# A hybrid three-group encoder layer: the second group's V projection in 512-column matmuls over two token tiles by turns, later differential steps, and moved loads

## The chip, the core and the metric

The kernel runs on one core of one Trainium2 chip. The metric is the device time of one launch in microseconds (us); the median of the runs is quoted. The core has five engines that run their own instruction queues in order and meet at semaphores: TensorE (PE; its weight loads appear as PEld), VectorE (DVE), ScalarE (ACT), GpSimd (POOL) and SyncE (SP), which here only issues DMAs. ScalarE's queue issues a few DMAs too (rows with ACTq).

## The reference

Two layers over x (512 tokens of width 1024, float32). In each layer the input is normalised and projected once; the columns of that projection belong to three head groups: A (differential attention, with rotary embedding on q and k), B (stick-breaking attention), C (forgetting attention with a cumulative gate).

```python
h = rms_norm(x, g_pre)
p = h @ w_in
qa, ka, va, ga, qs, ks, vs, gs, qf, kf, vf, gf, ff = jnp.split(p, split_at, axis=-1)
qa = apply_partial_rope(qa...); ka = apply_partial_rope(ka...)
ya = merge(diff_attention(qa, ka, heads(va), lam, lambda_init, subln)) * jax.nn.silu(ga)
yb = merge(stick_breaking_attention(heads(qs), heads(ks), heads(vs))) * jax.nn.silu(gs)
yc = merge(forgetting_attention(heads(qf), heads(kf), heads(vf), cum_log_f)) * jax.nn.silu(gf)
y = jnp.concatenate([ya, yb, yc], axis=-1) @ w_out
return x + rms_norm(y, g_post)
```

## The kernel before

Every large product is made of three matmuls (`mm3`, L200 to L202): each operand is held as a rounded high part and a low remainder, and high by high, high by low and low by high are summed in PSUM. The transposed normalised input `hT` is cut once per layer. Each weight unit (512 KB, `raw`) is loaded by SP, ScalarE writes its high part (`hl`, L184), and GpSimd writes the low part (L190) in four pieces of 256 columns; `split_to` does this, unit by unit, and four `hl` buffers (`whl_p`) and three `raw` buffers go round. The matmul of L201 is the one that reads the low part of a V unit.

The order of all work is written out by a planner: `do(cost, fn)` puts a piece of TensorE's main stream at the planner's own clock `now`, `at(t, fn)` puts other work (evictions, attention steps, splits, loads) at a time of that clock, and in the end everything is sorted by that time and emitted, each engine taking its instructions in that order. The planner's times (in ns) are only a sort key. The weights of a unit are split at its time of use less its `lead`.

In each layer the groups come in the order a, c, b: V first, then q and k for four pairs. While TensorE projects one group, the attention steps of the group before it are threaded in (`steps`): during c's projection those of a (`step_a`, the differential steps), during b's those of c, and those of b run during the gate projections. A differential step writes two score tiles in PSUM (`s`, two buffers, L364), VectorE takes their minimum (`mn`, L389) and so frees them, ScalarE takes the exponential (L398).

For the third group (b), V is projected by `proj_V`: four weight units of 256 rows by 512 columns, 512-column matmuls, one token tile of 128 after the other. For a and c it is `proj_N`: two column halves of 256, each of two units. For group a's q and k, VectorE applies the rotary embedding first (L328 to L332), ScalarE then writes the high part of q or k (L344) and VectorE the low part (L349).

After the last projection the output projection runs in two column halves; its first half is kept in `acc` tiles in PSUM and multiplied by the post-norm weights `gain` (L791); the second half runs token tile by token tile, and the next layer's pre-norm (`pre_norm_stages`: squares, two scalings, two transposes `turn`) is threaded in at five offsets after each tile.

Of the kernel before, what the change touches and what calls it, by code (L numbers as in the profile page):

```python
# [10 lines left out]
F32 = mybir.dt.float32  # L11
# [49 lines left out]
def hybrid_kernel(ctx, tc, x, w_in, forget_bias, diff_lambda, diff_subln, w_out, pre_norm, post_norm, consts, out):  # L61
# [137 lines left out]
    def mm3(ps, lh, ll, rh, rl, first, last):  # L199
        nc.tensor.matmul(out=ps, lhsT=lh, rhs=rh, start=first, stop=False)  # L200
        nc.tensor.matmul(out=ps, lhsT=lh, rhs=rl, start=False, stop=False)  # L201
        nc.tensor.matmul(out=ps, lhsT=ll, rhs=rh, start=False, stop=last)  # L202
# [33 lines left out]
        for t, fn in done(st):  # L236
            at(now[0] + t, fn)

    def proj_V(k0, tt, hT, done):

        st = {}
        sl = slice(tt * 128, (tt + 1) * 128)

        def go(q):
            if q == 0:
                st["ps"] = pj_p.tile([128, S], F32, name="pj", tag="pj")
            h = hT()
            for kc in range(2 * q, 2 * q + 2):
                u = halves[k0 + q]["hl"][:, :, kc % 2]
                mm3(st["ps"], h[0][:, kc, sl], h[1][:, kc, sl], u[:, 0], u[:, 1], kc == 0, kc == KC - 1)  # L250

        for q in range(4):
            do(1296, lambda q=q: go(q))
        at(now[0], lambda: done(st["ps"]))


    def pre_norm_stages(st, tt, hT):
# [56 lines left out]
        t = qk_p.tile([128, 2, S], F32, name="gain", tag="kd")  # L314
        return [t[:, 0], t[:, 1]]

    def load_gain(g, src):
        for h, t in enumerate(g):
            nc.sync.dma_start(out=t, in_=src[h * S:(h + 1) * S].partition_broadcast(128))


    H = (slice(0, 64), slice(64, 128))
# [267 lines left out]
    def first_norm(L):  # L590
        def load(tt):
            st = L["st", tt]
            t = qk_p.tile([128, 2, S], F32, name="xl", tag="qd")
            nc.sync.dma_start(out=t.rearrange("p h c -> p (h c)"), in_=x[0, tt * 128:(tt + 1) * 128, :])
            st["x"] = [t[:, 0], t[:, 1]]
            st["g"] = L.get("g")

        def first_gain():

            row = pt1_p.tile([1, 2, S], F32, name="grow", tag="pT1")  # L600
            nc.scalar.dma_start(out=row.rearrange("p h c -> p (h c)"), in_=pre_norm[0:1])
            one = t1_p.tile([1, 128], F32, name="one", tag="on")
            nc.vector.memset(one, 1.0)
            L["g"] = []
            for h in range(2):
                ps = s_p.tile([128, S], F32, name="s", tag="s")
                nc.tensor.matmul(out=ps, lhsT=one, rhs=row[:, h], start=True, stop=True)
                L["g"].append(ps)

        for tt in range(NT):  # L610
            L["st", tt] = {}
        t = -40000
        at(t, lambda: nc.vector.memset(mhalf, -0.5))
        at(t, lambda: load(0))
        at(t, first_gain)
        at(t, lambda: load_to(1))
        at(t, load_ident)
        at(t, lambda: L["st", 0].update(g=L["g"]))
        at(t, lambda: load_to(2))
        at(t, lambda: load(1))  # L620
        at(t, lambda: load(2))
        at(t, lambda: load_to(3))
        at(-20000, lambda: load(3))
        at(-19000, load_consts)
        S_ = [pre_norm_stages(L["st", tt], tt, L["hT"]) for tt in range(NT)]
        for t, tt, j in ((-30000, 0, 0), (-29900, 0, 1), (-29800, 0, 2), (-28000, 0, 3), (-27900, 0, 4), (-27000, 1, 0),
# [3 lines left out]
            at(t, S_[tt][j])  # L630

    def plan_layer(l, L):
# [9 lines left out]
        for g in ("a", "c", "b"):  # L642
            base = G[g]
            c = dict(pairs=[{} for _ in range(4)], lc=lc)
            st = {}
            c["v"] = lambda st=st: st["v"]
            c["o"] = lambda st=st: st["o"]
            c["cs"] = cs[l]
            t0 = now[0]
            at(t0, lambda st=st: st.update(v=v_p.tile([128, NT, 512], F32, name="v", tag="v")))  # L650
            if prev is not None:
                pst, pc, pg = prev
                at(t0, lambda pst=pst: pst.update(o=o_p.tile([128, 4, S], F32, name="o" + pg, tag="o")))
                steps(step_a if pg == "a" else step_c, pc, t0 + (3518 if pg == "a" else 3191), 50075 if pg == "a" else 46774)
            order = [(u, tt) for u in range(2) for tt in range(NT)]
            if g == "a":
                order = [(0, 0), (0, 1), (0, 2), (1, 0), (1, 1), (1, 2), (0, 3), (1, 3)]
            ks = []
            if g == "b":
                order = []  # L660
                kv = add_v_unit(l, base + 1024)
                for h in range(4):
                    use(kv + h, now[0] + 1296 * h)
                for tt in range(NT):
                    proj_V(kv, tt, hT, lambda ps, st=st, tt=tt: nc.scalar.activation(out=st["v"][:, tt], in_=ps, func=AF.Copy))
            for u in range(2 if g != "b" else 0):
                ks.append(add_in_unit(l, base + 1024 + u * UW, 6144 if g == "a" and u == 0 else None))
            seen = set()
            for u, tt in order:
                ex = g == "a" and u == 0  # L670
                w = UW + (8 if ex else 0)
                if u not in seen:
                    seen.add(u)
                    use(ks[u], now[0])
                    use(ks[u] + 1, now[0] + 1300)
                    if g == "a" and u == 1:
                        halves[ks[u]]["lead"], halves[ks[u] + 1]["lead"] = 7500, 6500

                def done(pst, u=u, tt=tt, ex=ex, st=st, w=w):
                    def ev():  # L680
                        nc.scalar.activation(out=st["v"][:, tt, u * UW:(u + 1) * UW], in_=pst["ps"][:, 0:UW],
                                             func=AF.Copy)
                        if ex:
                            if "ff" not in ffd:
                                ffd["ff"] = lay.tile([128, 32], F32, name="ff", tag="ff")
                            nc.vector.tensor_copy(ffd["ff"][:, tt * 8:(tt + 1) * 8], pst["ps"][:, UW:w])
                    return [(0, ev)]
                proj_N(ks[u], w, tt, hT, done)
            if g == "a":
                at(now[0] + 2000, lambda: layer_consts(lcd, l))  # L690
                at(now[0] + 5000, lambda: ffd.update(lf=decay(ffd["ff"], lcd, l)))
                at(now[0] + 9000, lambda: decay_sum(ffd["lf"], l))
            sc = 0.125 if g == "b" else -0.125
            for u in range(2):
                for part in ("q", "k"):
                    k0 = add_in_unit(l, base + u * UW + (512 if part == "k" else 0))
                    use(k0, now[0])
                    use(k0 + 1, now[0] + 2600)
                    if g == "a" and u == 0 and part == "q":
                        for h in range(2):  # L700
                            halves[k0 + h].update(lead=2500, lo="both")
                    if g == "b" and u == 0 and part == "q":
                        for h in range(2):
                            halves[k0 + h]["lead"] = (3800, 5100)[h]
                    for cc in range(2):
                        keep = c["pairs"][2 * u + cc]
                        if part == "q":
                            proj_T(k0, cc, hT, lambda pst, keep=keep: qk_done(pst, g == "a", sc, keep, "q"))
                        else:
                            proj_T(k0, cc, hT, lambda pst, keep=keep: qk_done(pst, g == "a", 1.0, keep, "k"))  # L710
            prev = (st, c, g)
            ctxs[g] = (st, c)
# [83 lines left out]
        def new_post():  # L796
            t = qk_p.tile([128, 2, S], F32, name="gain", tag="qs")
            gains["post"] = [t[:, 0], t[:, 1]]
            load_gain(gains["post"], post_norm[l])
        at(now[0] - 9000, new_post)  # L800
        N = None
        if l + 1 < DEPTH:
            nx = {}
# [13 lines left out]
        for tt in range(NT):  # L817
# [41 lines left out]
            at(t, square)  # L859
            at(t + 1867, add)  # L860
            if N is not None:
                for d, fn in zip((2500, 4500, 4600, 7551, 8326), pre_norm_stages(st, tt, N["hT"])):
                    at(t + d, fn)
        return N

# [50 lines left out]
```

## Time and profile before

| what | value |
|---|---|
| median of 3 runs | 869.72 us (869.27 to 870.09) |
| profiled execution, device time | 870.16 us |
| its span, first to last instruction | 868.1 us |
| mean granted TensorE clock | 0.998 |
| TensorE busy | 852.5 us, 98% of the span, 4700 matmuls |
| VectorE, ScalarE, GpSimd busy | 57%, 55%, 52% |

The table says where to look: TensorE is busy for all but some 16 us of the span, so a change counts by what it does to TensorE's own instructions and to its few waits. A busy share of an engine beside it says little by itself.

### The profile page before, as it was taken

Reading aid. Unit: us, or ns where it says so; the run is one execution under the profiler, and the core shown is the slowest. Engines: PE = TensorE matmul, PEld = TensorE weight load, DVE = VectorE, ACT = ScalarE, POOL = GpSimd, SP = SyncE. Lnnn points to the kernel's source line nnn. Section 1 sums busy time; section 2 is a strip of 40 time slices with the busy share of each in tenths; the row PEclk is TensorE's granted clock in tenths of the full one; section 3 lists DMA queues with packets and bytes.
Section 4 is the critical chain, followed back from the end, with each engine's and each line's share of the span. In section 5 each row is a group of like instructions: output and inputs, shape, how many; then the busy total and the mean of one; then the engine's idle time right before and its main releaser. Section 6 shows DMA issues by size and latency. Waiting matters only on the chain.

```text
span 868.1 us, 13536 instructions
## 1 busy us (share of the span) xinstructions
PE 852.5 (98%) x4700; PEld 711.0 (82%) x4700; DVE 496.4 (57%) x1143; ACT 475.9 (55%) x1056; POOL 447.7 (52%) x678
## 2 busy tenths in 40 slices
PE   7999999999999999999999999999999999999997
PEld 5988998888878787788898889888888787877885
DVE  5378656544555777623653875664445477774322
ACT  4344667757775556633334356675677756664310
POOL 3366554645544548770364664556274544678301
PEclk9999999999999999999999999999999999999999
DMA  7354323432523321237253452325244422122522
GB/s 236 96 163 134 94 81 91 118 101 80 154 76 105 85 61 53 71 117 247 96 177 98 122 146 74 98 73 162 59 131 113 120 54 71 49 81 89 167 100 97
DMA packets 71157, 94.24 MB, mean 109 GB/s; under 512 B 6433, under 2 KB 52129, under 8 KB 71090
## 3 DMA queue, kind: packets, MB, share of 16 engines
q1 hardware_dynamic: 68784, 89.19, 35.2%
q10 hardware_dynamic: 2306, 4.20, 1.6%
q8 instruction: 37, 0.61, 0.3%
q14 instruction: 30, 0.25, 0.1%
HBM read 76.56 MB, written 4.23 MB: 93 GB/s over the span
## 4 chain that ended last, share of the span: by engine, by line
PE 81%; DVE 10%; ACT 3%; DMA 2%; issue 2%; POOL 1%; DVEq 0%; POOLq 0%; ACTq 0%
PE pj L200 18%; PE pj L202 18%; PE pj L201 18%; PE s L364 7%; PE pt L372 5%; PE ov L462 5%; PE acc L200 2%; PE acc L202 2%; PE acc L201 2%; PE ov L424 2%; DVE ra L332 2%; DVE sh L331 2%; DVE sh L328 1%; DVE qd L349 1%; DVE ra L330 1%
## 5 line engine op out<-in xcount | busy, mean ns | idle before, releaser
L190 POOL TENSOR_TENSOR hl<-raw,hl 128x256 fp32r<-128x256 f32 (+1 forms) x418 | 341.1, 848 | 217.4 <-ACT hl L184 193.2
L200 PE MATMUL pj<-hT,hl 128*128 128x512 f32 x576 | 236.4, 410 | 0.0
L202 PE MATMUL pj<-hT,hl 128*128 128x512 f32 x576 | 225.7, 392 | 0.0
L201 PE MATMUL pj<-hT,hl 128*128 128x512 f32 x576 | 225.2, 391 | 0.0
L184 ACT ACTIVATE hl<-raw 128x1024 fp32r<-128x1024 f32 (+1 forms) x120 | 126.3, 1058 | 35.2 <-DMA raw<-in_w_out_dram 18.7
L202 PEld LDWEIGHTS pj<-hT,hl 128*128 128x128 f32 x576 | 108.1, 188 | 24.2
L200 PEld LDWEIGHTS pj<-hT,hl 128*128 128x128 f32 x576 | 108.4, 188 | 20.0 <-issue 2.1
L201 PEld LDWEIGHTS pj<-hT,hl 128*128 128x128 f32 x576 | 108.7, 189 | 17.0
L200 PE MATMUL pj<-hl,hT 128*128 128x256 f32 (+2 forms) x320 | 101.0, 316 | 0.3 <-ACT hT L282 0.2
L202 PE MATMUL pj<-hl,hT 128*128 128x256 f32 (+2 forms) x320 | 98.4, 308 | 0.5 <-DVE hT L283 0.5
L201 PE MATMUL pj<-hl,hT 128*128 128x256 f32 (+2 forms) x320 | 98.2, 307 | 0.0
L398 ACT ACTIVATE p<-p,mn 128x128 f32<-128x128 f32 (+3 forms) x128 | 71.0, 555 | 33.0 <-DVE mn L389 31.1
L531 DVE TENSOR_TENSOR_SCAN kp<-kp,c_masks 128x128 f32<-128x128 f32 (+3 forms) x64 | 67.3, 1051 | 18.6 <-ACT kp L524 18.1
L364 PE MATMUL s<-kd,qd 128*128 128x128 f32 (+1 forms) x192 | 61.9, 327 | 2.8 <-DVE mn L389 2.8
L200 PEld LDWEIGHTS pj<-hl,hT 128*128 128x128 f32 x320 | 61.4, 192 | 3.4 <-ACT hT L282 1.0
L202 PEld LDWEIGHTS pj<-hl,hT 128*128 128x128 f32 x320 | 61.1, 191 | 3.8 <-DVE hT L283 1.2
L375 ACT ACTIVATE pT<-pt 128x128 f32<-128x128 f32 (+3 forms) x96 | 41.2, 443 | 41.8 <-PE pt L372 41.6
L201 PEld LDWEIGHTS pj<-hl,hT 128*128 128x128 f32 x320 | 61.4, 192 | 2.6 <-POOL hl L190 0.6
L364 PE MATMUL s<-kd,qs 128*128 128x128 f32 (+1 forms) x192 | 61.1, 322 | 0.0
L536 DVE TENSOR_TENSOR sg<-sg,kp 128x127 f32<-128x127 f32 (+3 forms) x64 | 46.1, 720 | 5.5
L481 POOL TENSOR_TENSOR cm<-cb,c_causal 128x128 f32<-128x128 f32 x64 | 28.2, 461 | 38.6 <-DMA cb<-cs 21.2
L193 DVE TENSOR_TENSOR hl<-raw,hl 128x1024 fp32r<-128x1024 f32 (+3 forms) x18 | 21.4, 1199 | 44.7 <-ACT hl L184 44.5
(143 smaller groups left out, 1456.9 us busy)
## 6 DMA issues: line engine op xcount, KB each, us to landing
raw<-in_w_in_dram SPq DMA_DIRECT2D x96, 512.0 KB, 3.7
qs<-qd SPq DMA_DIRECT2D x48, 256.0 KB, 4.3
raw<-in_w_out_dram SPq DMA_DIRECT2D x24, 512.0 KB, 3.5
cb<-cs ACTq DMA_DIRECT2D x16, 256.0 KB, 3.2
xl<-in_x_dram SPq DMA_DIRECT2D x4, 512.0 KB, 5.4
xt<-in_x_dram SPq DMA_DIRECT2D x8, 256.0 KB, 6.3
xs<-xt SPq DMA_DIRECT2D x8, 256.0 KB, 2.0
xt<-xs SPq DMA_DIRECT2D x8, 256.0 KB, 2.8
```

The lines of the kernel that those rows point to most:

```text
L184: nc.scalar.activation(out=hl[:, 0], in_=raw, func=AF.Copy)
L190: nc.gpsimd.tensor_tensor(out=hl[:, 1, k, c:e], in0=raw[:, k, c:e], in1=hl[:, 0, k, c:e].bitcast(F32), op=ALU.subtract)
L200: nc.tensor.matmul(out=ps, lhsT=lh, rhs=rh, start=first, stop=False)
L201: nc.tensor.matmul(out=ps, lhsT=lh, rhs=rl, start=False, stop=False)
L202: nc.tensor.matmul(out=ps, lhsT=ll, rhs=rh, start=False, stop=last)
L364: nc.tensor.matmul(out=s[:, 0:n], lhsT=pr[q][:, m, i * 128:n], rhs=pr["k"][:, m, 0:n], start=(j == 0), stop=(j == 1))
L372: nc.tensor.transpose(out=pt[:, j * 128:(j + 1) * 128], in_=p[:, j * 128:(j + 1) * 128], identity=C["ident"])
L375: nc.scalar.activation(out=t, in_=src, func=AF.Copy)
L398: nc.scalar.activation(out=p[:, 0:n], in_=p[:, 0:n], func=AF.Exp, bias=st["mn", m], scale=-1.0, accum_out=su)
L462: nc.tensor.matmul(out=o[H[m], q0:256], lhsT=v[:, j, col:col + 64], rhs=ts[m][:, j, q0:256], start=(j == 0), stop=(j == i))
L531: nc.vector.tensor_tensor_scan(out=rv, data0=rv, data1=C["first"][:, S - n:S][:, ::-1], initial=0.0, op0=ALU.mult, op1=ALU.max)
L536: nc.vector.tensor_tensor(out=sg[:, 0:n - 1], in0=sg[:, 0:n - 1], in1=kp[:, 1:n], op=ALU.mult)
```

## The change

Five edits. (1) Group c's V takes the same path as b's: `proj_V`, 512 columns. (2) `proj_V` handles two token tiles by turns: tile one with units 0 and 1, tile two with units 0 and 1, then tile one with units 2 and 3, tile two with units 2 and 3; the leads of units 2 and 3 are set so that their splits fall where b's fell. The first q units of c get b's leads (3800 and 5100 in place of 9500 and 8000). (3) The differential steps begin at 6500 of c's stretch in place of 3518, and are spread over 47300 in place of 50075. (4) At the start the first norm weights (`grow`) are loaded by SP ahead of x in place of ScalarE's queue, and the identity is loaded ahead of the first weights. (5) The post-norm weights are loaded by ScalarE's queue, 3000 earlier, and the two `turn`s of the next layer's pre-norm stand some 950 later.

```diff
-    def proj_V(k0, tt, hT, done):
+    def proj_V(k0, tts, hT, done):
...
-        for q in range(4):
-            do(1296, lambda q=q: go(q))
-        at(now[0], lambda: done(st["ps"]))
+        for q in (0, 2):
+            for tt in tts:
+                for j in range(2):
+                    do(1296, lambda tt=tt, q=q + j: go(tt, q))
+                if q == 2:
+                    at(now[0], lambda tt=tt: done(ps[tt], tt))
...
-            nc.scalar.dma_start(out=row.rearrange("p h c -> p (h c)"), in_=pre_norm[0:1])
+            nc.sync.dma_start(out=row.rearrange("p h c -> p (h c)"), in_=pre_norm[0:1])
...
+        at(t, first_gain)
         at(t, lambda: load(0))
-        at(t, first_gain)
+        at(t, load_ident)
         at(t, lambda: load_to(1))
-        at(t, load_ident)
...
-                steps(step_a if pg == "a" else step_c, pc, t0 + (3518 if pg == "a" else 3191), 50075 if pg == "a" else 46774)
+                steps(step_a if pg == "a" else step_c, pc, t0 + (6500 if pg == "a" else 3191), 47300 if pg == "a" else 46774)
...
-            if g == "b":
+            if g != "a":
                 order = []
                 kv = add_v_unit(l, base + 1024)
+                by = 2
                 for h in range(4):
-                    use(kv + h, now[0] + 1296 * h)
-                for tt in range(NT):
-                    proj_V(kv, tt, hT, lambda ps, st=st, tt=tt: nc.scalar.activation(out=st["v"][:, tt], in_=ps, func=AF.Copy))
-            for u in range(2 if g != "b" else 0):
+                    if by == 2:
+                        halves[kv + h]["lead"] = (9500, 8000, 7700, 6400)[h]
+                    use(kv + h, now[0] + 1296 * (h + (2 if by == 2 and h > 1 else 0)))
+                for t_ in range(0, NT, by):
+                    proj_V(kv, range(t_, t_ + by), hT,
+                           lambda ps, tt, st=st: nc.scalar.activation(out=st["v"][:, tt], in_=ps, func=AF.Copy))
+            for u in range(2 if g == "a" else 0):
...
-                    if g == "b" and u == 0 and part == "q":
+                    if g != "a" and u == 0 and part == "q":
...
-            load_gain(gains["post"], post_norm[l])
-        at(now[0] - 9000, new_post)
+            load_gain(gains["post"], post_norm[l], nc.scalar)
+        at(now[0] - 12000, new_post)
...
-                for d, fn in zip((2500, 4500, 4600, 7551, 8326), pre_norm_stages(st, tt, N["hT"])):
+                for d, fn in zip((2500, 4500, 4600, 8500, 9275), pre_norm_stages(st, tt, N["hT"])):
```

How this moves instructions is read from the order of each engine's queue. First ScalarE where group a's last k projections are finished and c's V begins, before (`kd` is the high part of k, `hl` that of a weight unit; the first `hl` here is the first unit of V's second column half):

```order
L344 ACTIVATE kd<-ra 64x512 x2
L184 ACTIVATE hl<-raw 128x1024
L344 ACTIVATE kd<-ra 64x512 x2
L681 ACTIVATE v<-pj 128x256
L184 ACTIVATE hl<-raw 128x1024
L398 ACT_TABLE_LOAD
L398 ACTIVATE p,su_987<-p,mn_959 128x128
```

The same place of the changed kernel, where the two `hl` are V's third and fourth unit:

```order
L347 ACTIVATE kd<-ra 64x512 x2
L184 ACTIVATE hl<-raw 128x1024 x2
L347 ACTIVATE kd<-ra 64x512 x2
L401 ACT_TABLE_LOAD
L401 ACTIVATE p,su_974<-p,mn_966 128x128
L672 ACTIVATE v<-pj 128x512
```

Both late units stand between the last two `kd`, and the first V eviction stands behind the first exponential.

Next TensorE in c's V of the first layer, before, from the last matmuls of the first token tile on (`pj` are PSUM tiles, `hl_817` and `hl_845` the two units of the first column half, `s` a score tile):

```order
L200 MATMUL pj_903<-hl_845,hT0_145 128x256
L201 MATMUL pj_903<-hl_845,hT0_145 128x256
L202 MATMUL pj_903<-hl_845,hT1_146 128x256
L200 MATMUL pj_940<-hl_817,hT0_145 128x256
L201 MATMUL pj_940<-hl_817,hT0_145 128x256
...
L202 MATMUL pj_940<-hl_817,hT1_146 128x256
L364 MATMUL s_955<-kd_696,qd_594 128x128
L364 MATMUL s_955<-kd_696,qs_605 128x128
```

After, the same engine from the 24th matmul of c's V on (`hl_887` and `hl_918` are the third and fourth unit, the two that stand together in ScalarE's rows above):

```order
L202 MATMUL pj_935<-hl_845,hT1_146 128x512
L200 MATMUL pj_911<-hl_887,hT0_145 128x512
L201 MATMUL pj_911<-hl_887,hT0_145 128x512
...
L200 MATMUL pj_911<-hl_918,hT0_145 128x512
L201 MATMUL pj_911<-hl_918,hT0_145 128x512
L202 MATMUL pj_911<-hl_918,hT1_146 128x512
L367 MATMUL s_962<-kd_696,qd_594 128x128
L367 MATMUL s_962<-kd_696,qs_605 128x128
```

The third unit is read from the 25th matmul on and the fourth from the 31st, where before two units served the first 96; the first score stands behind the 36th 512-column matmul, where it stood behind the 36th 256-column one.

Last SP at the start, before:

```order
L594 DMA xl<-in_x_dram 128x1024
L175 DMA raw<-in_w_in_dram 128x4x256
L175 DMA raw<-in_w_in_dram 128x4x8
L106 DMA c_masks<-in_consts_dram 128x128
L175 DMA raw<-in_w_in_dram 128x4x256
```

and after:

```order
L604 DMA grow<-in_pre_norm_dram 1x1024
L597 DMA xl<-in_x_dram 128x1024
L106 DMA c_masks<-in_consts_dram 128x128
L175 DMA raw<-in_w_in_dram 128x4x256
L175 DMA raw<-in_w_in_dram 128x4x8
```

The first x load (`xl`) is the second DMA of the queue now, and the first weights the fourth.

## Rows read from the trace of the kernel before

**Rows 1.** The page: busy time, share of the span and instructions of each engine.

```profile
PE 852.5 (98%) x4700; PEld 711.0 (82%) x4700; DVE 496.4 (57%) x1143; ACT 475.9 (55%) x1056; POOL 447.7 (52%) x678
```

**Rows 2.** The waits of TensorE: us in total, times, longest.

```profile
PE s L364 <- DVE mn L389: 2.8, 2, 1.7
PE pt L279 <- DVE xn L273: 1.6, 2, 1.0
...
PE pj L200 <- DVE y L791: 0.2, 1, 0.2
```

**Rows 3.** Timeline of TensorE, c's V in both layers: start, us, instruction [idle before].

```profile
83.59 0.28 PE L200 MATMUL pj<-hl,hT 128*128 128x256 f32 x1
...
91.10 0.28 PE L202 MATMUL pj<-hl,hT 128*128 128x256 f32 x1
92.47 0.38 PE L364 MATMUL s<-kd,qd 128*128 128x256 f32 x1 [1.09 <-DVE mn L389]
...
508.39 0.28 PE L200 MATMUL pj<-hl,hT 128*128 128x256 f32 x1
...
512.71 0.22 PE L364 MATMUL s<-kd,qd 128*128 128x128 f32 x1
...
515.91 0.28 PE L202 MATMUL pj<-hl,hT 128*128 128x256 f32 x1
517.93 0.38 PE L364 MATMUL s<-kd,qd 128*128 128x256 f32 x1 [1.75 <-DVE mn L389]
```

**Rows 4.** Timeline of TensorE in b's V, first layer.

```profile
182.57 0.39 PE L200 MATMUL pj<-hl,hT 128*128 128x512 f32 x1
182.85 0.50 PE L201 MATMUL pj<-hl,hT 128*128 128x512 f32 x1
...
195.66 0.39 PE L201 MATMUL pj<-hl,hT 128*128 128x512 f32 x1
...
198.18 0.22 PE L364 MATMUL s<-kd,qd 128*128 128x128 f32 x1
```

**Rows 5.** Timeline of ScalarE at the end of a's k, both layers.

```profile
84.42 1.28 ACT L344 ACTIVATE kd<-ra 64x512 fp32r<-64x512 f32 x2 [3.24 <-DVE ra L332]
85.72 1.06 ACT L184 ACTIVATE hl<-raw 128x1024 fp32r<-128x1024 f32 x1
...
511.18 1.06 ACT L184 ACTIVATE hl<-raw 128x1024 fp32r<-128x1024 f32 x1
```

**Rows 6.** Timeline of GpSimd: low parts of units, and a small step of group a.

```profile
86.86 3.72 POOL L190 TENSOR_TENSOR hl<-raw,hl 128x256 fp32r<-128x256 f32 x4 [1.88 <-ACT hl L184]
...
116.19 0.19 POOL L125 TENSOR_SCALAR msub<-ssa 128x1 f32<-128x1 f32 x1 [4.44 <-ACT oj L432]
...
179.98 2.83 POOL L190 TENSOR_TENSOR hl<-raw,hl 128x256 fp32r<-128x256 f32 x4 [0.34 <-ACT hl L184]
...
512.32 3.73 POOL L190 TENSOR_TENSOR hl<-raw,hl 128x256 fp32r<-128x256 f32 x4 [1.89 <-ACT hl L184]
```

**Rows 7.** Timeline of VectorE, rotary embedding of a's last k.

```profile
87.79 1.05 DVE L331 SCALAR_TENSOR_TENSOR sh<-sh,rope 128x512 f32<-128x512 f32 x1
88.87 1.11 DVE L332 TENSOR_TENSOR ra<-ra,sh 128x512 f32<-128x512 f32 x1
90.68 1.40 DVE L349 SCALAR_TENSOR_TENSOR kd<-ra,kd 64x512 fp32r<-64x512 f32 x2 [0.70 <-ACT kd L344]
```

**Rows 8.** Timeline of SP's queue and of VectorE at the start.

```profile
0.72 0.39 SPq L594 DMA_DIRECT2D xl<-in_x_dram  x1
...
4.42 0.69 DVE L264 CUSTOM_DVE_ANT_0 xn<-xl 128x512 f32<-128x512 f32 x1 [3.42 <-DMA xl<-in_x_dram]
```

**Rows 9.** Timeline of ScalarE and TensorE between the layers.

```profile
391.82 1.06 ACT L184 ACTIVATE hl<-raw 128x1024 fp32r<-128x1024 f32 x1 [6.53 <-DMA raw<-in_w_out_dram]
...
438.36 0.39 PE L202 MATMUL pj<-hl,yq 128*128 128x512 f32 x1
439.40 0.63 PE L279 MATMUL pt<-c_masks,xn 128*128 128x128 f32 x4 [0.66 <-DVE xn L273]
```

More of the change, by code (lines that the diff above doesn't have):

```diff
@@ L237, in proj_N, with go @@
             at(now[0] + t, fn)
-    def proj_V(k0, tt, hT, done):
-        st = {}
-        sl = slice(tt * 128, (tt + 1) * 128)
-        def go(q):
+    def proj_V(k0, tts, hT, done):
+        ps = {}
+        def go(tt, q):
             if q == 0:
-                st["ps"] = pj_p.tile([128, S], F32, name="pj", tag="pj")
+                ps[tt] = pj_p.tile([128, S], F32, name="pj", tag="pj")
             h = hT()
+            sl = slice(tt * 128, (tt + 1) * 128)
             for kc in range(2 * q, 2 * q + 2):
                 u = halves[k0 + q]["hl"][:, :, kc % 2]
-                mm3(st["ps"], h[0][:, kc, sl], h[1][:, kc, sl], u[:, 0], u[:, 1], kc == 0, kc == KC - 1)
-        for q in range(4):
-            do(1296, lambda q=q: go(q))
-        at(now[0], lambda: done(st["ps"]))
+                mm3(ps[tt], h[0][:, kc, sl], h[1][:, kc, sl], u[:, 0], u[:, 1], kc == 0, kc == KC - 1)
+        for q in (0, 2):
[4 more added lines that the diff above has]
+                    at(now[0], lambda tt=tt: done(ps[tt], tt))
     def pre_norm_stages(st, tt, hT):
@@ L315, in new_gain, with load_gain @@
         return [t[:, 0], t[:, 1]]
-    def load_gain(g, src):
+    def load_gain(g, src, eng=nc.sync):
         for h, t in enumerate(g):
-            nc.sync.dma_start(out=t, in_=src[h * S:(h + 1) * S].partition_broadcast(128))
+            eng.dma_start(out=t, in_=src[h * S:(h + 1) * S].partition_broadcast(128))
     H = (slice(0, 64), slice(64, 128))
```

## The prediction

> **What bounds the kernel.** I read the page's busy shares first: TensorE is busy 852.5 us, 98% of the span [rows 1]. So the second view is the list of TensorE's own waits. Apart from the first load they are few: two of 2.8 us together for score tiles that VectorE has not yet read, 1.6 us for transposes of the normalised input, 0.2 us for a PSUM tile [rows 2]. The kernel is bound by TensorE's stream, and a change gains by (a) fewer or cheaper matmuls, (b) those waits, and loses by any new wait that it puts in front of a matmul. The third view is the timeline of TensorE where the change works, c's V in both layers, and beside it the queues of the two engines that feed it with weights.
>
> The sum is made on the profiled execution (870.16 us, span 868.1) as differences, and put on the median of the runs, 869.72, which is 0.44 lower. A change under 0.2% (1.74 us) is about what a measurement of this kernel cannot tell from none.
>
> **c's V in 512 columns.** TensorE starts 36 matmuls of 256 columns between 508.39 and 512.71, 0.120 us each [rows 3]. In b's V, from 195.66 to the score at 198.18, eleven matmuls of 512 columns start in 2.52 us, 0.229 each [rows 4]. Per layer 8 half tiles x 24 = 192 matmuls of 256 become 96 of 512: 192 x 0.120 - 96 x 0.229 = 23.0 - 22.0 = 1.05 us; two layers **-2.1** (bounds 1.7 and 2.5, a spacing 0.002 to either side).
>
> By the Trainium skill, page "TensorE: Matmul & The Clock Gate", section "Back-to-back issue gap", matmuls follow each other at columns over 2.4 GHz plus 2.5 ns, which is 109.2 and 215.8 ns; the gain would be 0.25 us a layer by that, 0.5 in all, and the total 1.6 us higher than mine. Here both spacings are in the trace, and it disagrees with both figures.
>
> **The score waits.** Before, the second step's score at 92.47 starts 1.37 us after the matmul at 91.10 where 0.12 is the rule, in the second layer 517.93 after 515.91, 2.02: 1.25 + 1.90 = 3.15 us [rows 3]. The cause is VectorE: until 92.08 it is busy with the last k of group a [rows 7] and only then reads the first score tiles. Starting the steps 2982 later puts the first score behind 36 matmuls of 512 columns, at 83.59 + 36 x 0.229 = 91.8 or later, and the second step's behind six more matmuls; VectorE is free by then. **-3.15**, bounds 2.8 and 3.35. The steps end at the same place (6500 + 47300 against 3518 + 50075, 0.2 apart), so what they add to b's stretch does not change.
>
> **The late weight units.** This is the new wait. The third unit of V is read from the 25th matmul on, the fourth from the 31st; before, two units fed the first 96 matmuls. Supply, first layer: ScalarE writes the third unit's high part where a V unit stood before, behind a `kd` that waits for VectorE, so from 85.72 [rows 5]. Its low part is GpSimd's, 86.86 to 90.58, 3.72 us for four pieces [rows 6]. The fourth unit's high part follows at once on ScalarE (to 87.9), but its low part starts only when GpSimd is done with the third, at 90.58. Such a unit takes 2.83 us where GpSimd is undisturbed (179.98) and 3.72 where two VectorE instructions whose two inputs are both in SBUF fall into it (L331, L332) [rows 6, 7]. From 90.68 VectorE runs L349 twice, with both inputs (`ra`, `kd`) in SBUF [rows 7]: the nearest row is 3.72, so the end is 94.30; undisturbed it would be 93.41. No row shows L349 beside a split.
>
> The Trainium skill, page "SBUF — State Buffer", section "Who interferes with whom", says that a VectorE instruction with two SBUF inputs and a GpSimd one that reads SBUF exclude each other for a whole instruction; that would give the later end too.
>
> Demand, first layer: V starts at 83.59 [rows 3], and the 35th matmul, the last that needs a fresh piece, would start at 83.59 + 34 x 0.229 = 91.38. It waits until 94.30: 2.92 us, in three pieces at the second half of the third unit and both halves of the fourth. Second layer: GpSimd 512.32 + 3.73 = 516.05 [rows 6], end 519.78, demand 508.39 + 7.79 = 516.18: 3.60 us. That TensorE goes on as each piece ends is seen in b's V: GpSimd ends a unit at 179.98 + 2.83 = 182.81, and the L201 that needs it starts at 182.85 [rows 4, 6]. Sum **+6.5**; undisturbed 2.03 + 2.71, **+4.75**. What stands behind on TensorE (scores, the second tile) moves back by the same; nothing there is late then.
>
> **b's V.** It waited a little for its fourth unit: 182.85 is 0.28 after 182.57, 0.05 over the spacing [rows 4]. By turns the unit is needed 2.7 us later: **-0.1** over two layers. c's q units are split later on the planner's clock; hidden by the last tiles of V (a rival below). Evictions of V become 4 of 512 columns in place of 8; ScalarE is off the path there.
>
> **Between the layers.** The transposes at 439.40 start 1.04 us after 438.36 where 0.229 would do [rows 9]; half a tile later (12 matmuls, 1.4 us) their input is there: **-0.8**. The post-norm weights come earlier: **-0.2** [rows 2]. Their two issues stand on ScalarE, at most some 0.4 us each by SP's issue [rows 8], in a stretch where it idles 6.5 us for a load [rows 9]: nothing.
>
> **The start.** x is behind one more issue on SP, 0.39 us and the step to the next: `xl` starts at about 1.16 in place of 0.72, and VectorE waits for nothing else at 4.42 [rows 8]. **+0.45**; bounds 0 (the load lands as before) and 0.9 (the first weights, now behind the identity, bind as well).
>
> **Sum.** -2.1 - 3.15 + 6.5 - 0.1 - 0.8 - 0.2 + 0.45 = +0.6: 869.72 + 0.6 = **870.3 us**. What the wider matmuls and the later scores give is taken by weights that come late. With all bounds one way it lies between 867.9 and 871.5, all but wholly inside 0.2%.
>
> **Rivals.** *B, the late units cost half or nothing.* For it: in b's V the same split places cost 0.05 us; the planner's clock gives the splits 7.7 and 6.4 us of lead. Against it: at the end of group a ScalarE runs behind its planned place, held by the rotary chain, which b's stretch does not have. Without the wait: 870.3 - 6.5 = 863.8; at half 867.1. Band 863.8 to 867.9, chance 0.30.
>
> *C, c's first q units come late; slower.* Their splits stand on ScalarE behind the second `oj` and on GpSimd behind the second `msub` of group a, and a `msub` has waited 4.44 us [rows 6]. A unit takes 1.06 + 2.83 = 3.9 us from ScalarE's start; the lead of 3800 is three pieces of six matmuls, 4.1 us, plus the attention matmuls among them. If the second `msub` is later than TensorE by more than that margin, each layer pays; 0.6 us per layer decides for slower, the longest wait seen gives 4.4 per layer, 879. Against it: b's q has had these leads, and no such wait stands in [rows 2]. 872 to 879, chance 0.17.
>
> *D, the wide matmuls bring nothing*: fed by turns they run at 0.240, twice the 256-column spacing. The 2.1 falls away, 872.4. Against it: 0.229 in b's V [rows 4]. Chance 0.03. It is what the page on TensorE comes near to.
>
> **Chances.** My forecast 0.50 (867.9 to 871.5), B 0.30, C 0.17, D 0.03. Faster by over 0.2%: 0.30; within: 0.50; slower: 0.20. The range takes the forecast whole, the upper half of B and the near part of C and D, some 0.8: 865.2 to 872.6.
>
> **What will show it.** In the profile after: waits of L201 in c's V for GpSimd's low parts, some 3 us per layer near 90 to 94 and 514 to 520, and no more waits of scores for `mn` there; GpSimd's fourth unit ending near 94.3; 0.229 spacing in c's V; the first `xn` at about 4.9; no wait of transposes at 439. I am wrong if those L201 waits are absent or under 1.5 us per layer (B), or if L200 to L202 of c's first q wait for GpSimd (C).

## The result, and the profile after

The changed kernel takes **881.73 us** (median of 4), against 869.7 in the same comparison: ratio 1.014, interval 1.0128 to 1.0152. I had forecast 870.3 and a range up to 872.6; it is 12 us slower, above the range and on a side to which I gave 0.20.

The page, busy time of each engine, answers to [rows 1]:

```profile
PE 854.8 (97%) x4508; PEld 700.7 (80%) x4508; DVE 495.1 (56%) x1143; ACT 475.2 (54%) x1048; POOL 447.3 (51%) x678
```

TensorE issues 192 matmuls fewer, its busy time (in which the ends of matmuls are modelled) is 2.3 us higher, and its share a point lower. The loss shows in its waits; the list answers to [rows 2]. In it `p` is the weight tile of a differential step, `wT` its transpose, `on` the step's output, and `oc` the transposed output that VectorE reads from PSUM, after which TensorE may transpose the next one (`pt`).

```profile
PE pj L201 <- POOL hl L190: 4.7, 7, 0.9
PE pt L375 <- DVE p L417: 4.4, 6, 0.9
PE pt L443 <- DVE oc L444: 2.9, 4, 0.7
PE s L610 <- DMA grow<-in_pre_norm_dram: 2.5, 1, 2.5
PE pj L200 <- ACT hT L285: 1.3, 3, 0.8
PE pt L375 <- ACT wT L378: 1.2, 2, 0.6
PE pt L282 <- DVE xn L276: 0.9, 1, 0.9
PE pj L202 <- DVE hT L286: 0.4, 2, 0.2
```

The score waits for `mn` are gone, and the first row is the wait for late weights, both as forecast. The rows for `p`, `oc` and `wT`, 8.5 us together, are new, and no step of the prediction has them.

Where the time went is read from where TensorE starts the same work. c's stretch (start of c's V to start of b's V) is 93.82 us before and 100.25 after in the first layer, 94.50 and 100.21 in the second; c's V starts 1.14 later in the first layer (84.73 for 83.59); from b's V to c's V of the second layer it is 330.98 before and 329.46 after. +1.14 + 6.43 - 1.52 + 5.71 = 11.76; the two spans differ by 11.7.

TensorE by windows, first layer after: c's V, c's q and k, b's V. The columns are the window, its length, the busy time (matmul records), the granted clock as a share of full speed, the DMA share and GB/s.

```profile
84.73:115.40 30.67, 28.44 (x142) 1.00 0.21 58
115.40:184.98 69.58, 65.26 (x349) 1.00 0.40 109
184.98:214.80 29.82, 29.82 (x159) 1.00 0.22 66
```

c's q and k before:

```profile
115.14:177.41 62.27, 62.27 (x337) 1.00 0.39 105
```

In c's q and k TensorE now stands still for 4.3 of 69.6 us; before, the 62.27 us of that stretch were all busy. Some 12 matmuls of the steps stood in c's V before and stand in this stretch now, so not all of the 7.3 us between the two is loss. The granted clock is 1.00 in every one of these windows and explains nothing of it.

The late units, TensorE and GpSimd in c's V, answer to [rows 3, 6]:

```profile
84.73 0.39 PE L200 MATMUL pj<-hl,hT 128*128 128x512 f32 x1
84.96 0.39 PE L201 MATMUL pj<-hl,hT 128*128 128x512 f32 x1
85.19 0.39 PE L202 MATMUL pj<-hl,hT 128*128 128x512 f32 x1
...
90.85 0.39 PE L200 MATMUL pj<-hl,hT 128*128 128x512 f32 x1
91.75 0.50 PE L201 MATMUL pj<-hl,hT 128*128 128x512 f32 x1 [0.51 <-POOL hl L190]
...
93.57 0.50 PE L201 MATMUL pj<-hl,hT 128*128 128x512 f32 x1 [0.86 <-POOL hl L190]
...
95.40 0.50 PE L201 MATMUL pj<-hl,hT 128*128 128x512 f32 x1 [0.86 <-POOL hl L190]
```

```profile
87.98 7.36 POOL L190 TENSOR_TENSOR hl<-raw,hl 128x256 fp32r<-128x256 f32 x8 [1.88 <-ACT hl L184]
```

The spacing is 0.227, and there are three waits for GpSimd, at the three places forecast; the last ends as GpSimd's eighth piece ends (87.98 + 7.36 = 95.34).

The new wait, first of its kind: VectorE, and under it TensorE, in c's q.

```profile
118.08 0.35 DVE L417 SCALAR_TENSOR_TENSOR p<-p,rho 128x128 f32<-128x128 f32 x1
121.81 0.35 DVE L430 TENSOR_SCALAR on<-ov,r 128x128 f32<-128x128 f32 x1 [3.38 <-PE pt L443]
...
123.03 0.91 DVE L417 SCALAR_TENSOR_TENSOR p<-p,rho 128x256 f32<-128x256 f32 x1
```

```profile
118.41 1.05 PE L427 MATMUL ov<-v,wT 128*128 128x128 f32 x8
...
121.50 0.27 PE L443 MATMUL pt<-c_masks,on 128*128 128x128 f32 x1
...
124.08 0.41 PE L375 MATMUL pt<-c_masks,p 128*128 128x128 f32 x2 [0.93 <-DVE p L417]
125.21 0.33 PE L443 MATMUL pt<-c_masks,on 128*128 128x128 f32 x1 [0.72 <-DVE oc L444]
```

The `ov` that L430 reads is finished at 119.46, yet L430 starts at 121.81, just after TensorE's transpose L443 at 121.50. L443 does not produce what L430 reads: it reads an older `on`, and L430 writes the next `on`. So VectorE waits for a buffer. Behind L430 in its queue stands the next step's combine (L412 to L417), which ends at 123.94, and TensorE's transposes of that step (L375) wait for it.

### The profile page after: what moved, and what is told of

Read it like the earlier page. It is cut to its first block, busy times and chain, and to the rows that moved or that the text cites. A ratio compares the mean times of both kernels' runs of the same rounds, so it can differ in the third digit from the quotient of the medians.

```text
span 879.8 us, 13143 instructions
## 1 busy us (share of the span) xinstructions
PE 854.8 (97%) x4508; PEld 700.7 (80%) x4508; DVE 495.1 (56%) x1143; ACT 475.2 (54%) x1048; POOL 447.3 (51%) x678
## 4 chain that ended last, share of the span: by engine, by line
PE 80%; POOL 9%; issue 5%; DVE 3%; ACT 1%; DMA 1%; SPq 0%; DVEq 0%; POOLq 0%; ACTq 0%
PE pj L200 18%; PE pj L202 18%; PE pj L201 18%; POOL hl L190 9%; PE s L367 7%; PE pt L375 5%; PE ov L465 4%; PE acc L200 2%; PE acc L202 2%; PE acc L201 2%; PE ov L427 2%; DMA raw<-in_w_in_dram 1%; DVE p L417 1%; PE pt L282 1%; ACT hl L184 1%
## 5 line engine op out<-in xcount | busy, mean ns | idle before, releaser
L200 PE MATMUL pj<-hT,hl 128*128 128x512 f32 x576 | 236.4, 410 | 0.0
L202 PE MATMUL pj<-hT,hl 128*128 128x512 f32 x576 | 225.7, 392 | 0.0
L201 PE MATMUL pj<-hT,hl 128*128 128x512 f32 x576 | 225.3, 391 | 0.0
L202 PEld LDWEIGHTS pj<-hT,hl 128*128 128x128 f32 x576 | 108.1, 188 | 24.2
L200 PEld LDWEIGHTS pj<-hT,hl 128*128 128x128 f32 x576 | 108.6, 189 | 20.1 <-issue 2.1
L201 PEld LDWEIGHTS pj<-hT,hl 128*128 128x128 f32 x576 | 108.7, 189 | 16.8
L201 PE MATMUL pj<-hl,hT 128*128 128x512 f32 (+2 forms) x256 | 88.2, 345 | 4.7 <-POOL hl L190 4.7
L200 PE MATMUL pj<-hl,hT 128*128 128x512 f32 (+2 forms) x256 | 90.4, 353 | 1.3 <-ACT hT L285 1.3
L202 PE MATMUL pj<-hl,hT 128*128 128x512 f32 (+2 forms) x256 | 87.7, 343 | 0.4 <-DVE hT L286 0.4
L201 PEld LDWEIGHTS pj<-hl,hT 128*128 128x128 f32 x256 | 49.4, 193 | 11.2 <-POOL hl L190 7.6
L200 PEld LDWEIGHTS pj<-hl,hT 128*128 128x128 f32 x256 | 49.5, 194 | 6.8 <-ACT hT L285 2.1
L202 PEld LDWEIGHTS pj<-hl,hT 128*128 128x128 f32 x256 | 49.3, 192 | 5.9 <-DVE hT L286 0.9
L125 POOL TENSOR_SCALAR msub<-ssa 128x1 f32<-128x1 f32 x32 | 9.4, 295 | 75.0 <-ACT oj L435 74.1
```

## The experiments

Times of all runs are medians beside the kernel before on the same chip (869.9 to 870.2 there); in brackets stands the 95% interval of the ratio to it.

**The q leads.** My first theory after the result: c's two q units, split back to back on GpSimd (112.38 to 117.99) ahead of a `msub`, hold the steps up.

```
-                    if g != "a" and u == 0 and part == "q":
+                    if g == "b" and u == 0 and part == "q":
```

> The changed kernel with the split places of c's first q units as before (both split later by the planner's default, instead of 3800 and 5100 ahead). Theory Q (the two q units, split back to back on GpSimd from 112.4 to 118.0, push the third msub and with it the combine of the differential steps behind TensorE): TensorE's waits for p and for oc in the stretch of c's q and k, 8.5 us over both layers, go, and the time falls from 881.7 to 873 to 875. Rival S (the steps, begun later and packed denser, run behind by themselves): those waits stay, the time stays within 2 us of 881.7. If half of each is true: 877.

885.32 us (1.016 to 1.019): slower still, with TensorE's waits for `p` at 5.4 and for `oc` at 2.9. The expectation has the direction of the edit wrong: with leads of 9500 and 8000 the two units are split earlier, not later (their low parts begin at 105.72 and 110.68, apart from each other). Theory Q falls all the same, and with it the prediction's rival C: the new leads of q help.

**Start and spread of the steps**, undone in the changed kernel, and made alone in the kernel before.

```
-steps(... t0 + (6500 if pg == "a" ...), 47300 if pg == "a" ...)
+steps(... t0 + (3518 if pg == "a" ...), 50075 if pg == "a" ...)
```

> The changed kernel with the differential steps begun and spread as before (3518 and 50075). Theory S (later and denser steps are what TensorE waits for in c's q and k projections): the waits of transposes for p, for oc and for wT, 8.5 us in all, go, the score waits for mn return in part (up to 3.2 us), time 873 to 877. Rival Q (the q units on GpSimd): the waits for p and oc stay, the time is 881 to 885 with the score waits on top.

869.16 us (0.9982 to 1.0008), better than the 873 to 877 expected. The waits for `p`, `oc` and `wT` are gone, those for `mn` are 3.9. Undoing this one line gives all of the 12 us back.

> The kernel before with one edit, the differential steps begun at 6500 and spread over 47300. Theory S: the waits of transposes for p and oc appear here too, 4 us per layer less the score waits of 3.15 in all: 873 to 876. Rival Q: only the score waits go, 866.5 to 868.

877.48 us (1.0071 to 1.0105): 7.6 slower, more than I expected, with no other edit. Theory S holds by the time alone: the only trace of this run is of an execution of 1714.84 us, and no rows of it are read.

Then each of the two numbers for itself:

> The changed kernel with the steps begun at 6500 but spread as before, over 50075: later, not denser. Theory D (density: at the smaller spacing the parts of a step that come 8 to 17 planned us after its start fall on other parts of later steps, and VectorE stands behind a transpose that TensorE does not reach): the waits of transposes for p and oc go, what stays is the wait for V's late units: 873 to 876. Rival L (lateness: the projections that cover the steps lie otherwise): the waits stay, 879 to 882.

> The changed kernel with the steps begun as before, at 3518, but spread over 47300: denser, not later. Theory D: the waits for p and oc appear with the score waits, 874 to 878. Rival L: the time of the kernel with start and spread as before, 868 to 870.

875.28 us (1.005 to 1.008) and 877.84 (1.0071 to 1.0105). The smaller spacing brings the waits for `oc` (3.7) and `p` (2.2) back beside the score waits; the late start has 4.7 of late units, which no score wait covers any more, and 3.2 for `on` and `p`. Against the run with both undone, 869.16, that is 6.1 for the late start and 8.7 for the density: both matter, and together (12.6) they are less than the sum.

**The last part of the step.** A step's `on` tile is written 7856 after the step's start and read for the last time at 17029.

```
-                      (7856, av), (8256, square), (9775, norm), (17029, back)):
+                      (7856, av), (8256, square), (9775, norm), (16085, back)):
```

> The changed kernel with one number changed in the differential step: its last part (the transpose back of the normalised output) comes 16085 after the step's start in place of 17029, as the spacing of the steps is smaller by the same ratio. Theory B (the last part of an older step, in front of the next combine on VectorE, is what holds p and oc up): 8.5 us of waits go but for 1 to 2, 874 to 876. Rival: other parts collide too, the waits stay within 2 us of 8.5, 880 to 883.

871.48 us (1.0008 to 1.0027): one number gives 10.2 us back, more than expected. TensorE's waits for `p` are 0.3, for `oc` none. Its c stretch, the windows of the same three parts as above:

```profile
84.27:114.94 30.67, 28.44 (x141) 1.00 0.21 59
114.94:179.15 64.21, 64.06 (x348) 1.00 0.45 122
179.15:208.83 29.68, 29.68 (x158) 1.00 0.20 57
```

c's V is the same to the hundredth, b's V to 0.14; the q and k are 5.37 shorter, and so they are in the second layer (69.57 and 64.20). So what this number governs costs 5.4 us per layer, 10.7 in all.

**The buffer.** The edit above does two things: it shortens the life of `on`, and it moves the transposes in TensorE's queue. This one gives `on` a fourth buffer and moves no instruction:

```
-    t1_p = P("t1", 3)
+    t1_p = P("t1", 4)
```

> The changed kernel with four buffers for the normalised output tile (on) in place of three, nothing else. Theory N (a step's on lies from 7856 to 17029 after its start, 9173, and with the spacing of 47300 / 16 = 2956 a step lasts 3.1 spacings, so the fourth on waits on VectorE for a transpose that stands far back on TensorE; with 50075 it is 2.9): VectorE's waits of L430 for L443, 38.0 us, all but go, TensorE's waits for p and oc fall from 7.3 us to under 1, the time from 881.7 to 871 to 873. Rival O (the place of the last part in the queues, not the buffer: the 16085 version moved both): the waits stay, 880 to 882.

874.39 us (1.0027 to 1.0048), 7.3 better, though above the 871 to 873 expected; its ten runs lie in two groups, 871.8 to 873.0 and 874.3 to 875.2, of which the last section tells. VectorE's waits at L430, and TensorE's:

```profile
DVE on L430 <- PE ov L427: 26.9, 18, 3.1
```

```profile
PE pt L443 <- DVE oc L444: 1.2, 2, 0.7
...
PE pt L375 <- DVE p L417: 0.5, 2, 0.3
```

For comparison, VectorE's waits for that buffer in the changed kernel, with the last part at 16085, and (by the line numbers of before) in the kernel before:

```profile
DVE on L430 <- PE pt L443: 38.0, 16, 4.5
```

```profile
DVE on L430 <- PE pt L443: 12.5, 8, 3.4
```

```profile
DVE on L427 <- PE pt L440: 17.7, 12, 4.5
```

With the fourth buffer L430 waits only for its input, `ov`. c's q and k in this run, first and second layer:

```profile
115.71:180.42 64.71, 63.94 (x348) 1.00 0.44 120
542.12:607.24 65.12, 64.06 (x348) 1.00 0.44 120
```

They are 4.87 and 4.45 shorter than in the changed kernel: 9.3 of the 10.7 us are the buffer, and theory N holds for these. The other 1.4 go only when the last part is moved too; 1.7 us of waits for `oc` and `p` are left here.

How far three buffers reach is not told by the mean spacing. In the planner's times, the life of an `on`, 9173, is 3.1 mean spacings of 47300 / 16 = 2956 and 2.9 of 3130, but the steps of a head stand 0.7, 0.9, 1.1 and 1.3 mean spacings apart (`W_STEP` in the kernel), so a fourth `on` comes 2.7, 3.3, 3.1 or 2.9 of them behind the first. At 2956 that is 7982, 9755, 9164 and 8573: three of four are shorter than the life, one of them by only 9. At 3130 two are (8450 and 9076), and at 2956 with the life of 8229 one is (7982). VectorE waits 16, 12 and 8 times in these three versions, and with 16085 only at each head's last step, as this count has it. So three buffers are short in all three, and only for the first do the runs show a price of some size in TensorE's time.

> The kernel before with four on buffers. Its spacing is 2.9 steps, VectorE waits 17.7 us for the buffer, but TensorE for none of it: 869.9, no change. If the buffer held the kernel before up as well: 866 to 868.

869.88 us (0.9986 to 1.0005), no change: in the kernel before VectorE waits 17.7 us for the buffer, and TensorE loses nothing by it.

**A start in whole pieces.** Main work goes out in pieces of six matmuls, so I tried whether a start later by two whole pieces is free:

```
-steps(... t0 + (6500 if pg == "a" ...), 47300 if pg == "a" ...)
+steps(... t0 + (6110 if pg == "a" ...), 50075 if pg == "a" ...)
```

> The changed kernel with the steps spread as before (50075) and begun at 6110, which is 3518 and two pieces of six matmuls, in place of 6500. Theory P (what decides is where the parts of a step fall between the pieces of six matmuls, so a start moved by whole pieces costs nothing): the waits for p and for on that the start at 6500 shows with this spread, 3.2 us, go, 872 to 873, and only V's late units stay (4.7 us). Rival (the late start itself costs): 875 to 876, as with 6500.

875.37 us (1.0038 to 1.0074), as with 6500 (875.28). The waits for `on` and `p` did fall, from 3.2 to 1.8, c's stretch from 96.47 to 95.33 in the first layer; but a score wait of 0.9 appeared in b's V in each layer (at 188.30 in the first). There VectorE cannot read c's first score before GpSimd has made the mask `cm`: it starts at 187.94 here, and at 188.00 with 6500, where TensorE came to its next score only at 188.36.

```profile
187.94 0.29 DVE L392 CUSTOM_DVE_ANT_0 p<-s,cm 128x128 f32<-128x128 f32 x1 [3.00 <-POOL cm L484]
```

Theory P was half right; its gain in c's stretch did not reach the time, and the new score wait is one place where it went.

**The late units.** The third unit's high part ahead of the first `kd` on ScalarE:

```
-                        halves[kv + h]["lead"] = (9500, 8000, 7700, 6400)[h]
+                        halves[kv + h]["lead"] = (9500, 8000, 8500, 7500)[h]
```

> The changed kernel with the third unit of V split ahead of the first kd of group a on ScalarE (8500 and 7500 ahead in place of 7700 and 6400). The term of the late units: GpSimd goes on to the third unit at 85 or 86 in place of 88, so the waits of L201 for it shrink from 4.7 us to 1 to 2, and the time by as much, 878 to 879. Rival: what follows (the first scores, behind VectorE's last k) takes the time in their place, 881 to 882.

879.62 us (1.0096 to 1.0126), 2.1 better (2.7 to 3.7 was expected). GpSimd now runs three units without a break:

```profile
82.28 11.10 POOL L190 TENSOR_TENSOR hl<-raw,hl 128x256 fp32r<-128x256 f32 x12 [1.89 <-ACT hl L184]
```

One wait of 0.84 per layer is left in c's V, for the last half of the fourth unit (GpSimd ends at 93.38).

**The start**, undone in the changed kernel and made alone in the kernel before:

```
-            nc.sync.dma_start(out=row..., in_=pre_norm[0:1])
+            nc.scalar.dma_start(out=row..., in_=pre_norm[0:1])
...
-        at(t, first_gain)
         at(t, lambda: load(0))
-        at(t, load_ident)
+        at(t, first_gain)
         at(t, lambda: load_to(1))
+        at(t, load_ident)
```

> The changed kernel with the start as before: the first gain row on ScalarE's queue, the identity behind the first weights, x ahead of both. If TensorE's lag of 1.14 us at the start of c's V (84.73 against 83.59) is all from the moved loads and carries through to the end: 880.6. Rival: the waits behind it absorb it (they are set by GpSimd and VectorE, whose work does not begin earlier): 881.7, no change.

883.22 us (1.0139 to 1.0184), no gain in the time, although c's V starts 1.28 earlier, at 83.45. In its profiled execution the granted clock fell behind the late units, to a mean of 0.95 and 0.90 over c's V in the two layers; c's V is 1.65 and 3.07 longer there than in the changed kernel, more than the start. Inconclusive.

> The kernel before with the start of the changed one alone: the first gain row on SP's queue ahead of x, the identity ahead of the first weights. The prediction's term 0.45 gives 870.3; the lag of TensorE in the changed kernel's trace, 1.14, gives 871.0; if later waits absorb it, 869.9, as before.

871.16 us (0.9998 to 1.0017): 1.2 more, which the interval cannot tell from nothing. The trace says by what: VectorE starts on `xl` at 4.50 in place of 4.42 [rows 8], but ScalarE's first weights come 2 us later. ScalarE before, and in this run:

```profile
6.29 1.08 ACT L184 ACTIVATE hl<-raw 128x1056 fp32r<-128x1056 f32 x1 [1.15 <-DMA raw<-in_w_in_dram]
```

```profile
8.26 1.08 ACT L184 ACTIVATE hl<-raw 128x1056 fp32r<-128x1056 f32 x1 [3.04 <-DMA raw<-in_w_in_dram]
```

c's V starts 0.65 later here, at 84.24.

**What is left of the change**: steps and start as before, V and the loads and places between the layers as changed.

> The changed kernel with steps and start as before: V in 512 columns, its leads, and the loads and places between the layers are left. By the prediction's terms without the late units' wait, which the score wait hides here: 869.9 - 2.2 - 1.0 = 866.7, and 867.2 if the late units cost 0.4 to 0.9 as with the steps back alone; by that run (869.2) and the start alone (+1.2): 868.0.

869.33 us (0.9974 to 0.9993), above all three times expected; four of its ten runs are at 867.7 to 868.1, where the last of the three is. The score waits are 3.9, and no wait for late units appears in c's V. The two waits lie over each other, and the score wait covers the late units.

**Versions that beat both.** Last part at 16085, units early, start as before; the same with four buffers in place of 16085; and with steps at 6110 over 50075:

> The changed kernel with three edits: the last part of the differential step 16085 after its start, V's third unit split ahead of the first kd (8500, 7500), and the start's loads as before. By the single runs: 881.7 - 10.2 - 2.1 - 1.1 = 868.3; if the start brings nothing, 869.4. Rival (the terms share a wait, the scores behind VectorE's last k take the place of the late units): 870 to 871.

> The changed kernel with four on buffers (the last part at 17029 as it is), V's third unit split ahead of the first kd (8500, 7500), and the start's loads as before. Theory N: as good as the version with 16085, 865.9, within 0.7 either way. Rival O: 876 to 878.

> The changed kernel with the steps at 6110 over 50075, V's third unit split ahead of the first kd (8500, 7500) and the start's loads as before. By theory P: 872.5 - 2.1 - 1.1 = 869.3, or 1 to 2 us less where the wait that the start at 6110 leaves is smaller than thought; by its rival 872 to 873.

**865.86 us** (0.9931 to 0.9964), 867.66 (0.9961 to 0.9984) and 867.29 (0.9956 to 0.9979). The first is 0.53% faster than the kernel before, and 2.4 us better than the single runs added up to. The second does not come as near to it as expected (within 0.7): with four buffers the last part stays where it was, and the waits for `oc` (1.2) and `p` (0.5) with it. c's V and c's q and k in the first:

```profile
83.67:112.49 28.82, 27.98 (x142) 1.00 0.24 63
112.49:176.69 64.20, 64.04 (x349) 1.00 0.45 122
```

Together they take 93.02 us, 0.80 less than before: with `on` released sooner the later, denser steps no longer cost more than the score waits that they remove.

## Why the prediction was wrong, step by step

- **The step that failed** is a sentence, not a term: the steps end at the same place, "so what they add to b's stretch does not change", and behind the late units "nothing there is late then". Start and end were looked at, the spacing between was not, and the cost of denser steps stood at nothing. The spacing shrinks from 3130 to 2956, and three of four `on` tiles then live longer than three buffers allow, where two of four did. VectorE stands still at L430 for 38.0 us in place of 17.7, the combine behind it is late, TensorE waits: 5.4 us per layer, 10.7 in the sum where I had nothing. The fourth buffer shows 9.3 of it to be the buffer; the rest goes with the place of the last part. With the score waits it gives the single edit: 869.9 - 3.15 + 10.7 = 877.5, measured 877.48. That run has no rows, so the agreement is one of totals, and part of it may be luck.
- **The score waits, -3.15**: right in the changed kernel, where no wait for `mn` is left. Wide matmuls alone do not remove them (3.9 with the steps back).
- **The late units, +6.5**: right in place and cause, and nearly in size: 5.9. The last waiting matmul starts 95.40 - 84.73 = 10.67 after V's start, 34 x 0.227 = 7.72 without waits: 2.95 (forecast 2.92); second layer 525.08 - 514.44 = 10.64: 2.92 (forecast 3.60, because GpSimd began 3.93 behind V's start there before and begins 3.23 behind it now). So rival B is out. GpSimd was slowed by VectorE's last `kd` as taken for the later end: eight pieces take 7.36, 0.92 each, where 2.83 / 4 = 0.71 is undisturbed [rows 6], and the two L352 in them 2.26, where [rows 7] had 1.40. The Trainium skill, "SBUF — State Buffer", "Who interferes with whom", has these two kinds of instruction contend, and the trace agrees in that both take longer; that one excludes the other for a whole instruction no row here shows. But the term does not add to the score waits: with the early steps the score wait covers the late units.
- **c's V in 512 columns, -2.1**: right, 0.227 makes it 192 x 0.120 - 96 x 0.227 = 1.25 per layer, 2.5. Rival D is out.
- **b's V, -0.1**: nothing speaks against it; six of the seven L201 waits are c's (4.42 of 4.7 us), the seventh (0.28) is at the start.
- **Between the layers, -1.0**: right in kind, the trace has 1.52 less from b's V to the next layer's c's V, and no transposes wait there any more.
- **The start, +0.45**: the forecast's own step, `xl` 0.44 later, did not come: `xl` is issued 0.41 later, but VectorE starts on it only 0.09 later. The mechanism of the upper bound came true and went past it: the first weights are 2 us late, as in the run of the start alone, and c's V starts 1.14 late. What it costs in time is open (1.2 in that run, which its interval does not tell from nothing).
- **Rival C** had the right side and the wrong cause: no L200 to L202 of c's q waits, and taking the leads away costs 3.6 us.
- **The lower end of the forecast** is mis-added: with all bounds one way, c's V at -2.5 among them, the sum is -2.2, which gives 867.5 and not 867.9. Nothing hangs on it here.

With these sizes c's first stretch should be longer by -1.25 - 1.25 + 2.95 + 5.37 = 5.8, the second by -1.25 - 1.90 + 2.92 + 5.37 = 5.1. Measured are 6.43 and 5.71; some 0.6 us per layer stay unexplained. They do not lie in c's V: added from start to start, waits included, its matmuls take 25.31 us in the second layer (25.56 before) and all others of the stretch 74.91 (68.94 before), 6.0 more where 5.37 are explained. With 16085 the others of the first layer still take 69.54, so the 0.6 is with the later, denser steps too; by what is open.

## What to carry to other kernels

When work is packed denser, list for each rotating buffer how long one tile lives, and compare it with the shortest stretch of as many steps as there are buffers, not with the mean: where the life is longer, a queue stops though no dependence of data asks for it. Whether that costs time shows only in the waits of the engine that bounds the kernel: here VectorE's 17.7 us for the `on` buffer cost nothing before, and said that the margin was thin. Two waits at one place can cover each other, so a term for each is not a sum.

## What the runs showed of the hardware

A wait of TensorE is at times followed by a stretch at the lower of its two clock levels (1.2 in place of 2.4 GHz, a granted clock of 0.50). In the run with steps and start back, windows (us, busy, granted clock) and TensorE's rows behind the score wait:

```profile
83.41:93.10 9.69, 7.71 (x35) 1.00 0.43 117
93.10:96.40 3.30, 3.22 (x10) 0.50 0.46 124
96.40:116.43 20.03, 20.03 (x110) 1.00 0.04 14
```

```profile
93.18 0.58 PE L367 MATMUL s<-kd,qd 128*128 128x256 f32 x1 [1.97 <-DVE mn L392]
...
94.20 0.63 PE L200 MATMUL pj<-hl,hT 128*128 128x512 f32 x1
94.63 0.63 PE L201 MATMUL pj<-hl,hT 128*128 128x512 f32 x1
...
96.64 0.39 PE L200 MATMUL pj<-hl,hT 128*128 128x512 f32 x1
96.87 0.40 PE L201 MATMUL pj<-hl,hT 128*128 128x512 f32 x1
```

The 512-column matmuls start 0.43 apart in place of 0.23 for some 3 us, and then at full speed again. In the second layer of the same execution c's V has its score wait too, and the clock stays at 1.00. Of this kernel's ten runs six are at 869.3 to 869.6 (mean clock 0.996 or 0.997), four at 867.7 to 868.1 (0.999): 1.6 us, the second price of a wait. The traces with 16085 and with four buffers have one such stretch each, in c's V of the second layer, which is 1.6 us longer there than in the changed kernel (32.26 and 32.27 for 30.64). The four runs of the best version, with one wait of 0.84 per layer in c's V, lie between 865.8 and 866.15.
